# Hybrid mLSTM / attention step on one core: a run's additions placed behind the last plain tile, and the first sample state three ticks later

## The chip, the cores and the metric

The kernel runs on one core of a Trainium2 chip. The core has a matrix engine (TensorE, PE in the profile; its weight loads are shown as PEld), VectorE (DVE), ScalarE (ACT), GpSimd (POOL) and SyncE (SP), whose queue issues most of the transfers between DRAM and the on-chip memory. Each engine works through its own instructions in a fixed order; semaphores make it wait for the others. The metric is the device time of one execution in microseconds. Times of a kernel are given as the median of several runs; the profile is of one further execution.

## The reference

One layer of a decoder is computed for 512 prompt positions and 32 sample positions (8 sequences of 4), 544 columns in all, with model width 2048. All arithmetic is in float32.

- u = x w_in gives q, k, v, o and z of the mLSTM branch (4 heads of width 512), q, k, v and z of a sliding-window attention branch, two merge gates and the input and forget gates.
- For the samples, each of the 8 sequences has a state C (512 x 512 for each head), which is read and updated. In the reference this is, for a chunk,

```
num = einsum('bhts,bhsd->bhtd', s, v) + inter * einsum('bhtk,bhkv->bhtv', q, C)
C_new = decay * C + einsum('bhsk,bhsv->bhkv', w * k, v)
```
- Each branch is normalised and gated (br_m, br_a), then y = sigmoid(g_m) * (br_m w_proj_m) + sigmoid(g_a) * (br_a w_proj_a), and the result is the layer norm of alpha * x + y w_out. The new states are outputs too.

## The kernel before, in words

**Products in float32.** PE multiplies in a narrower format. A weight tile of 128 x 1024 (half of the depth of one column tile) is loaded as `raw`, ScalarE casts it to the high part `wh` (L200) and VectorE subtracts, `wl = raw - wh` (L201, both in `split`). The activations have such parts too. A product is made of high x high, high x low and low x high. Buffers: three of `raw`, two of each of `wh` and `wl`.

**Plain column tiles** (`gemm`, `products`, matmuls at L209): two halves, in each 8 steps of the depth, with three products on two column halves of 272: 48 matmuls for each half. In each step of the depth the matmuls with `wh` come first, then the one with `wl`.

**Runs of pairs** (`paired`, L697). Two column tiles are computed with a seven-product scheme of the Strassen-Winograd kind: seven steps n = 0 to 6, each with 16 matmuls on a `wh` (L664) and 8 on a `wl` (L666). The weight operands of the steps are sums of the four quarter blocks b11, b12, b21, b22 of the weights. `prepare` makes them up to three steps ahead, at raised scheduling priority: in n = 1 it adds t1 = b11 + b12, in n = 2 it adds b11 = t1 + b22 (both VectorE, L644), other sums are made by accumulating transfers of POOL (L642); then it splits the sum. `gather` combines the seven results. There are three runs: one for w_in (about 102 to 1785 us), one for w_proj_m (from about 2160) and one for w_out (from about 2337). Ahead of the second and the third, four column tiles go through plain `gemm`; while these run, `operand_sums` makes the sums of the activations for the run behind them (L1548 to L1551 and the casts and subtractions L243, L244 on s1, n2, n3, s4), and `merge` (L1577, L1578) multiplies finished plain tiles by the gate.

**Ticks.** Each step of a run of pairs, and each part of a plain gemm, ends with `tick()`, which moves a list of generators on by one `yield`. One of them is `samples()`, which works through the samples of the mLSTM heads during the first run.

**The sample chain.** For each head, `sample_prep` loads q, k, v, replicates them (L1087, L1110), transposes them on PE (L1096, L1115), writes the scaled k and the v through a DRAM buffer (`d_kv`, L1060) and loads them back in another layout as KB (L1066) and VB (L1067); nT (L1127, L1129) and the normaliser's products (L1133) are made here too. Then `sample_head` (L1173) takes the eight states: POOL masks KB into Ab (L1192), some ticks pass (`for j in range(4 + b % 2): yield`, L1197), in which the stores of the last state and the loads of the next C are issued; PE multiplies the masked q by C (L1211, four matmuls) and Ab by VB (L1216, four), at a priority that puts them ahead of other work of that tick; VectorE updates C (L1218, four). `sample_finish` normalises (L1162, L1169) and stores the head to `d_brm` (L1171). When the last of four heads is through, `samples()` closes its buffers and loads the 16 tiles `pf` of the attention branch (L1246), which are split into bh and bl (L243, L244).

**After the first run** the plain gemm of w_proj_a multiplies these bh and bl, with the prompt's mLSTM (`mlstm`, whose d_v, d_k and d_q loads are at L1463) between its ticks, up to about 2070 us; then come the four plain tiles of w_proj_m and the second run.

**What sets the order.** A scheduler lays the program's instructions out on each engine by priority and by the order in which the program issues them; `tc.high_priority(offset=n)` moves a block forward, and `tc.issue_after(ins)` puts what is traced in its block behind `ins` in the order of the engine of `ins`.

Of the kernel before, what the change touches and what calls it, by code (L numbers as in the profile page):

```python
# [18 lines left out]
ALU = mybir.AluOpType  # L19
# [55 lines left out]
def _build(tc, nc, i, o, es):  # L75
# [11 lines left out]
    V, A, G, PE = nc.vector, nc.scalar, nc.gpsimd, nc.tensor  # L87
# [13 lines left out]
    def nm(s):  # L101
        count[0] += 1
        return f"{s}_{count[0]}"
# [7 lines left out]
    def r32(ap):  # L111
        return ap.bitcast(F32)
# [13 lines left out]
    state = {}  # L126

    def tick():

        with ExitStack() as place:  # L130
            if state.get("end"):
                place.enter_context(tc.issue_after(state["end"].ins))
            for g in list(live):
                if next(g, StopIteration) is StopIteration:
                    live.remove(g)
# [58 lines left out]
    def split(raw, p=None, tags=("wh", "wl"), parts=1):  # L194
        p = p or wp
        wh = p.tile([128, 8, 128], F32R, tag=tags[0], name=nm("wh"))
        wl = p.tile([128, 8, 128], F32R, tag=tags[1], name=nm("wl"))
        n = 8 // parts
        for k in range(0, 8, n):
            A.copy(wh[:, k:k + n], raw[:, k:k + n])  # L200
            V.tensor_tensor(out=wl[:, k:k + n], in0=raw[:, k:k + n], in1=r32(wh[:, k:k + n]), op=ALU.subtract)  # L201
        return wh, wl

    def products(ps, half, wh, wl, xh, xl, cols, every=8):
# [110 lines left out]
    for g in range(8):  # L315
        for q in range(2):
            k = g * 2 + q
# [311 lines left out]
    def load_a(w):  # L629
        w["b11"], w["b12"] = (load_half(w["wv"], c0, 0) for c0 in (w["cA"], w["cB"]))  # L630

    def load_b(w):
        for n, c0 in (("b22", w["cB"]), ("b21", w["cA"])):
            w[n] = raw2()
            state["load"] = nc.sync.dma_start(w[n][:], w["wv"][:, 8:16, c0:c0 + 128])

    def prepare(w, n):


        def add(out, a, b):  # L640
            if w.get("acc") and out == a and n != 2:
                G.dma_start(out=w[out][:], in_=w[b][:], accum_op=ALU.add)  # L642
            else:
                V.tensor_tensor(out=w[out][:], in0=w[a][:], in1=w[b][:], op=ALU.add)  # L644
        if n == 1:
            w["t1"] = raw2()
            add("t1", "b11", "b12")
        elif n == 2:
            add("b11", "t1", "b22")
        w["hl", n] = split(w[("b11", "t1", "b11", "b21", "b12", "b22", "b21")[n]])  # L650
        if n == (1 if w.get("acc") else 3):
            add("b12", "b12", "b22")
        elif n == (3 if w.get("acc") else 4):
            add("b21", "b21", "b11")

    def half_product(w, n):
        if n < 3:
            w["bank", n] = bank()
        ps = w["bank", BANK[n]][:, :HT]
        wh, wl = w.pop(("hl", n))  # L660
        x, first = w["x"][n], n in (0, 1, 2)
        for k in range(8):
            for p in range(2):
                PE.matmul(ps, wh[:, k], x(p, k), start=(first and k == 0 and p == 0), stop=False, skip_group_check=True)  # L664
        for k in range(8):
            state["end"] = PE.matmul(ps, wl[:, k], x(0, k), start=False, stop=(k == 7), skip_group_check=True)  # L666

    def gather(w, n):

        A0, D0, B0 = (w["bank", b][:, :HT] if ("bank", b) in w else None for b in range(3))  # L670
        sc = w["scale"]
        if n == 0:
            w["p1"] = pe_.tile([128, HT], F32, tag="p1", name=nm("p1"))
            A.activation(w["p1"][:], A0, AF.Copy, scale=sc)
            return
        if n == 1:
            w["O1"], w["O2"] = ev(), ev()
        c11, c21 = (w["O1"][:, c:c + HT] for c in (0, HT))
        c12, c22 = (w["O2"][:, c:c + HT] for c in (0, HT))
        p1 = w["p1"][:]  # L680
        if n == 1:
            A.activation(c11, D0, AF.Copy, scale=sc)  # L682
            G.tensor_tensor(out=c22, in0=p1, in1=c11, op=ALU.subtract)  # L683
        elif n == 2:
            V.scalar_tensor_tensor(c12, B0, sc, p1, op0=ALU.mult, op1=ALU.subtract)
        elif n == 3:
            A.activation(c11, A0, AF.Copy, scale=sc)
        elif n == 4:
            V.scalar_tensor_tensor(c22, B0, -sc, c22, op0=ALU.mult, op1=ALU.add)  # L689
        elif n == 5:  # L690
            V.scalar_tensor_tensor(c12, D0, sc, c12, op0=ALU.mult, op1=ALU.add)
        else:
            V.scalar_tensor_tensor(c21, B0, sc, p1, op0=ALU.mult, op1=ALU.subtract)

    AHEAD = 400

    def paired(work):  # L697

        steps = [(w, n) for w in work for n in range(7)]
        ready = 0  # L700
        with tc.issue_after(state["load"].ins):
            load_a(work[0])
            load_b(work[0])
        for at, (w, n) in enumerate(steps):

            while ready < min(at + 3, len(steps)):
                with tc.high_priority(offset=AHEAD):
                    prepare(*steps[ready])
                ready += 1
            p = at // 7 + 1  # L710
            if p < len(work):
                if n == 3:
                    load_a(work[p])
                elif n == 4:
                    load_b(work[p])
            if n == 2 and "early" in w:
                w["early"]()
            half_product(w, n)
            with tc.high_priority(offset=AHEAD):
                gather(w, n)  # L720
            if n == 6:
                w["end"](w["O1"], w["O2"])
            tick()
# [346 lines left out]
    def load_C(h, b):  # L1070
        ct = sp["sC"].tile([128, 4, 512], F32, tag="C", name=nm("C"))
        nc.sync.dma_start(ct[:], i["state_mlstm_C"][b, h].rearrange("(c p) v -> p c v", p=128))
        return ct
# [99 lines left out]
    def sample_head(h):  # L1173
        r = {}
        nxt = load_C(h, 0)
        yield from sample_prep(h, r)
        pC, stores = None, []

        def store():

            with tc.issue_after(state["load"].ins):
                for dst, src in stores:
                    nc.sync.dma_start(dst, src)
            stores.clear()

        for b in range(NB):
            ct = nxt

            if b % 2 == 0:
                kb, vb = r["kv"]  # L1190
            Ab = st1([128, 128], "Ab", F32R, "sw")
            masked = G.tensor_scalar(Ab[:], r32(kb[:]), cc[:, C_M2 + b % 2:C_M2 + b % 2 + 1], None, op0=ALU.mult)  # L1192
            qz = st1([128, 4, NS], "qz", p="sw")
            with tc.issue_after(masked.ins):
                G.memset(qz[:], 0.0)
            G.tensor_copy(qz[:, :, b * 4:b * 4 + 4], r["qs"][:, :, b * 4:b * 4 + 4])
            for j in range(4 + b % 2):  # L1197
                yield
                if j == 0:
                    store()  # L1200
                elif j == 2 and b + 1 < NB:
                    with tc.issue_after(state["load"].ins):
                        nxt = load_C(h, b + 1)
                        if b % 2:
                            r["kv"] = load_kv(h, b // 2 + 1)
            if b == 0:
                pC = bank()

            with tc.high_priority(offset=3000):
                for c in range(4):  # L1210
                    PE.matmul(pC[c * 32:c * 32 + 32, :], qz[:, c], ct[:, c],  # L1211
                              start=(b == 0), stop=(b == NB - 1), tile_position=(0, c * 32))
                pus = [sm() for _ in range(4)]
                for c in range(4):
                    own = slice(c * 32, c * 32 + 32)
                    PE.matmul(pus[c][:], Ab[own], vb[own], start=True, stop=True, tile_position=(c * 32, 0))  # L1216
            for c in range(4):
                V.scalar_tensor_tensor(ct[:, c], ct[:, c], dcb[:, h, b:b + 1], pus[c][:], op0=ALU.mult, op1=ALU.add)  # L1218
                if c % 2:
                    stores.append((C_s[b, h, (c - 1) * 128:c * 128 + 128, :].rearrange("(c p) v -> p c v", p=128),  # L1220
                                   ct[:, c - 1:c + 1]))
            yield
        yield
        store()
        while h not in gated:
            yield
        yield from sample_finish(h, r, pC)
# [597 lines left out]
    for g in range(G3):  # L1825
# [13 lines left out]
        for half, raw in enumerate(raws):  # L1839
            wh, wl = (w[:, :, g] for w in w3[half])  # L1840
# [54 lines left out]
```

## Time and profile before

| | |
|---|---|
| median of 3 runs | 2493.77 us (2491.63 to 2494.89) |
| the profiled execution | 2497.55 us, its span 2495.7 us |
| TensorE busy | 2453.8 us (98% of the span) |
| VectorE busy | 1817.8 us (73%) |
| ScalarE busy | 1244.1 us (50%) |
| mean granted clock of TensorE | 0.995 |
| moved by DMA | 464.71 MB, mean 186 GB/s |

How to read the rows below. A row of waits names the engine, its operation and what it waited for, then the sum in us, how often, and the longest. A row of a timeline has the start in us from the beginning of the span, the busy time in us of the instructions grouped in it, the engine, the line, the operation, output and inputs with their shape, and the count; square brackets hold the idle time of the engine in front of it and what ended it. Matmuls overlap, so the distance between starts, not the busy time, is their pace. A row of windows has the stretch, its length, the busy time of PE, PEld, DVE, ACT and POOL with instruction counts, the granted clock, the share of the DMA engines and GB/s. A row for one line or tile has the count, the least, median and greatest duration in ns, and the first and last start.

### The profile page before, as it was taken

What the parts mean: (1) busy time and instruction counts of PE and PEld (TensorE: products, weight loads), DVE (VectorE), ACT (ScalarE), POOL (GpSimd) and SP (SyncE); (2) the same over time, 40 slices, a digit from 0 to 9 for tenths busy, and PEclk for the clock granted to TensorE, in tenths of its full rate; (3) what the DMA queues carried; (4) which work ended last, traced back from release to release, by engine and by line L of the source; (5) the groups of instructions that cost most, each with busy time, mean ns of one, the idle gap of its engine ahead of it and who ended that gap; (6) DMA issues with size and microseconds to landing.
All of it is one profiled execution on the core that took longest, in us unless ns stands there. A gap on an engine that the chain in (4) does not pass through costs nothing. (4 is left out here: it accounts for less than half of the span.)

```text
span 2495.7 us, 48772 instructions
## 1 busy us (share of the span) xinstructions
PE 2453.8 (98%) x19542; PEld 2394.0 (96%) x19542; DVE 1817.8 (73%) x2785; ACT 1244.1 (50%) x2033; POOL 373.1 (15%) x376
## 2 busy tenths in 40 slices
PE   8999999999999999999999999999999999999997
PEld 8999999999999999989999999999999999999997
DVE  7867677677677677777878788878855654666667
ACT  6457677667667665433433444444633333334431
POOL 2111121121111111121021121210000000110111
PEclk9999999999999999999999999999999999999999
DMA  6677666656666655468678677677755546788776
GB/s 166 154 185 187 150 151 159 158 144 163 153 152 156 151 128 151 106 204 243 205 216 243 167 232 240 188 225 226 251 171 172 189 149 205 198 229 258 213 220 190
DMA packets 557172, 464.71 MB, mean 186 GB/s; under 512 B 45328, under 2 KB 454080, under 8 KB 556688
## 3 DMA queue, kind: packets, MB, share of 16 engines
q1 hardware_dynamic: 540048, 402.07, 54.4%
q0 software_dynamic: 15696, 57.15, 11.8%
q8 instruction: 154, 2.52, 0.4%
q10 hardware_dynamic: 1200, 2.36, 0.3%
q14 instruction: 74, 0.61, 0.1%
HBM read 319.06 MB, written 96.31 MB: 166 GB/s over the span
## 5 line engine op out<-in xcount | busy, mean ns | idle before, releaser
L200 ACT CAST wh<-raw 128x1024 fp32r<-128x1024 f32 x632 | 661.9, 1048 | 814.6 <-PE bank L664 663.8
L201 DVE TENSOR_TENSOR wl<-raw,wh 128x1024 fp32r<-128x1024 f32 x632 | 778.9, 1234 | 222.7 <-ACT wh L200 203.4
L664 PE MATMUL bank<-xk,wh 128*128 128x272 f32 x2336 | 325.0, 290 | 0.9 <-DVE ev L689 0.9
L644 DVE TENSOR_TENSOR raw<-raw,raw 128x1024 f32<-128x1024 f32 x238 | 304.5, 1280 | 17.3 <-DMA raw<-in_w_in 8.2
L664 PEld LDWEIGHTS bank<-xk,wh 128*128 128x128 f32 x2336 | 304.3, 189 | 4.2 <-issue 2.6
L683 POOL TENSOR_TENSOR ev<-p,ev 128x272 f32<-128x272 f32 x82 | 124.8, 1522 | 674.1 <-ACT ev L682 613.7
L666 PE MATMUL bank<-xk,wl 128*128 128x272 f32 x1168 | 172.4, 288 | 0.8 <-DVE wl L201 0.8
L664 PE MATMUL bank<-s1h,wh 128*128 128x272 f32 x656 | 169.1, 291 | 0.2 <-ACT wh L200 0.2
L664 PE MATMUL bank<-n3h,wh 128*128 128x272 f32 x656 | 169.1, 289 | 0.0
L664 PE MATMUL bank<-n2h,wh 128*128 128x272 f32 x656 | 168.2, 289 | 0.6 <-ACT wh L200 0.6
L664 PE MATMUL bank<-s4h,wh 128*128 128x272 f32 x656 | 168.3, 290 | 0.1
L664 PE MATMUL bank<-n3l,wh 128*128 128x272 f32 x656 | 167.9, 287 | 0.0
L664 PE MATMUL bank<-n2l,wh 128*128 128x272 f32 x656 | 167.5, 287 | 0.0
L664 PE MATMUL bank<-s1l,wh 128*128 128x272 f32 x656 | 167.2, 287 | 0.0
L664 PE MATMUL bank<-s4l,wh 128*128 128x272 f32 x656 | 167.0, 287 | 0.0
L666 PEld LDWEIGHTS bank<-xk,wl 128*128 128x128 f32 x1168 | 156.6, 188 | 1.1 <-DVE wl L201 1.0
L664 PE MATMUL bank<-a11h,wh 128*128 128x272 f32 x584 | 150.8, 290 | 2.6 <-ACT wh L200 2.5
L209 PE MATMUL bank<-bh,wl 128*128 128x272 f32 x704 | 148.5, 291 | 4.7 <-DVE wl L201 4.7
L664 PE MATMUL bank<-a11l,wh 128*128 128x272 f32 x584 | 149.6, 289 | 0.0
L209 PE MATMUL bank<-bh,wh 128*128 128x272 f32 x704 | 148.8, 290 | 0.0
L209 PE MATMUL bank<-bl,wh 128*128 128x272 f32 x704 | 148.6, 290 | 0.0
L664 PEld LDWEIGHTS bank<-n3h,wh 128*128 128x128 f32 x656 | 123.3, 188 | 1.9 <-issue 1.4
(488 smaller groups left out, 5515.4 us busy)
## 6 DMA issues: line engine op xcount, KB each, us to landing
raw<-in_w_in SPq DMA_DIRECT2D x296, 512.0 KB
raw<-raw POOLq DMA_DIRECT2D x90, 512.0 KB, 5.0
C<-in_state_mlstm_C SPq DMA_DIRECT2D x32, 1024.0 KB
out<-C SPq DMA_DIRECT2D x64, 512.0 KB
raw<-in_w_proj_a SPq DMA_DIRECT2D x32, 512.0 KB
raw<-in_w_proj_m SPq DMA_DIRECT2D x32, 512.0 KB
raw<-in_w_out SPq DMA_DIRECT2D x32, 512.0 KB
d_v<-ev SPq DMA_DIRECT2D x16, 272.0 KB
```

The source lines that it names most:

```text
L200: A.copy(wh[:, k:k + n], raw[:, k:k + n])
L201: V.tensor_tensor(out=wl[:, k:k + n], in0=raw[:, k:k + n], in1=r32(wh[:, k:k + n]), op=ALU.subtract)
L209: PE.matmul(ps[f][:, :w], a[:, kk], b(k, c, w), start=(k == 0 and n == 0), stop=(k == 15 and n == 2))
L644: V.tensor_tensor(out=w[out][:], in0=w[a][:], in1=w[b][:], op=ALU.add)
L664: PE.matmul(ps, wh[:, k], x(p, k), start=(first and k == 0 and p == 0), stop=False, skip_group_check=True)
L666: state["end"] = PE.matmul(ps, wl[:, k], x(0, k), start=False, stop=(k == 7), skip_group_check=True)
L683: G.tensor_tensor(out=c22, in0=p1, in1=c11, op=ALU.subtract)
```

## The change

There are two edits.

1. `split` keeps its last subtraction in `state["split"]`. `paired` reads it on entry, when it is the subtraction of the last half of the last plain tile, and wraps `prepare` in `tc.issue_after` of that instruction. The additions and subtractions that `prepare` issues on VectorE stand behind it.
2. In `sample_head` the loop of ticks in front of the state's matmuls has 7 passes instead of 4 for the first state of the first head (`h + b == 0`). All other states keep 4 or 5.

```
-            V.tensor_tensor(out=wl[:, k:k + n], in0=raw[:, k:k + n], in1=r32(wh[:, k:k + n]), op=ALU.subtract)
+            state["split"] = V.tensor_tensor(out=wl[:, k:k + n], in0=raw[:, k:k + n], in1=r32(wh[:, k:k + n]),
+                                             op=ALU.subtract)
...
-        ready = 0
+        ready, plain = 0, state["split"]
...
-                with tc.high_priority(offset=AHEAD):
+                with tc.high_priority(offset=AHEAD), tc.issue_after(plain.ins):
                     prepare(*steps[ready])
...
-            for j in range(4 + b % 2):
+            for j in range(7 if h + b == 0 else 4 + b % 2):
                 yield
```

## The prediction, on record before the changed kernel ran

> **What bounds the kernel now.** I read the page first, then the list of what TensorE waited for, then the timelines of each engine round the longest waits.
>
> ```profile
> span 2495.7 us, 48772 instructions
> PE 2453.8 (98%) x19542; PEld 2394.0 (96%) x19542; DVE 1817.8 (73%) x2785; ACT 1244.1 (50%) x2033; POOL 373.1 (15%) x376
> ```
> PE works 2453.8 of 2495.7 us. The change removes no PE work (it moves instructions only), so it can win only in the 41.9 us that PE idles and in work done at a lower clock. The waits of PE say where (the start of the kernel and the tail behind the last matmul, which the change leaves alone, are left out here; us in total, times, longest):
>
> ```profile
> PE sm L1216 <- DMA VB<-d_kv: 5.4, 2, 5.1
> PE bank L209 <- DVE wl L201: 4.7, 2, 4.0
> PE bank L666 <- DVE wl L201: 0.8, 1, 0.8
> PE sm L1133 <- DVE nT L1129: 0.8, 1, 0.8
> ```
> The first two rows hold the two places that the change touches, 9.1 us. The other two are the next in size on its path, 0.8 us each.
>
> **Part 1: the run's additions behind the last plain tile's subtraction.** TensorE and VectorE just ahead of the second run of pairs (w_proj_m), from their timelines:
>
> ```profile
> 2147.64 0.41 PE L209 MATMUL bank<-bl,wh 128*128 128x272 f32 x2
> 2152.07 0.82 PE L209 MATMUL bank<-bh,wl 128*128 128x272 f32 x2 [4.02 <-DVE wl L201]
> 2152.69 0.66 PE L209 MATMUL bank<-bh,wh 128*128 128x272 f32 x2
> 2157.17 0.41 PE L209 MATMUL bank<-bl,wh 128*128 128x272 f32 x2
> 2159.92 0.29 PE L664 MATMUL bank<-bh,wh 128*128 128x272 f32 x1
> ```
> ```profile
> 2144.09 0.44 DVE L244 TENSOR_TENSOR n3l<-tx,n3h 128x272 fp32r<-128x272 f32 x1
> 2148.61 1.23 DVE L644 TENSOR_TENSOR raw<-raw,raw 128x1024 f32<-128x1024 f32 x1 [4.08 <-DMA raw<-in_w_proj_m]
> 2149.75 0.78 DVE L1577 TENSOR_TENSOR c<-bank,c 128x272 f32<-128x272 f32 x2
> 2150.45 0.43 DVE L1551 TENSOR_TENSOR tx<-tx 128x272 f32<-128x272 f32 x1
> 2150.80 1.22 DVE L201 TENSOR_TENSOR wl<-raw,wh 128x1024 fp32r<-128x1024 f32 x1
> ```
> ```profile
> 2143.74 1.05 ACT L200 CAST wh<-raw 128x1024 fp32r<-128x1024 f32 x1
> ```
> VectorE stands idle 4.08 us in front of the addition L644 (t1 = b11 + b12), which waits for a weight load; behind it in the queue stand L1577, L1551 and the subtraction L201 whose wl PE needs from 2148.05 on. The wh of that half was ready at 2144.79. In the changed kernel's VectorE order this one L644 stands behind that L201. Then L1577, L1551 and L201 follow n3l: 2144.5 + 0.7 + 0.35 + 1.2 = 2146.8 us, 1.2 us before PE wants wl. The 4.02 us go. The clock goes with them: from 2152.07 to 2157.17 the spacing of matmul pairs is 0.45 us instead of 0.25. Those 11 pairs take 5.10 us and would take 11 x 0.25 = 2.76, so 2.3 us more. **Part 1: -6.3 us.**
>
> What is late next: L644 itself still ends at 2149.8, and behind it the split of n=0 (buffers free at about 2148, wh to 2149.1, wl to 2151.0). PE would begin the run at 2159.92 - 6.3 = 2153.6 and need n=0's wl 2 us later and t1's split 3 us later; so 2 us or more are spare. In the third run (w_out) the same move of one L644 is made where PE has no gap, worth nothing; in the first run VectorE's order stays. No DMA and no instruction of SP, POOL, ACT or PE moves by part 1.
>
> The Trainium skill, "TensorE: Matmul & The Clock Gate", section "Part 1: The HAM clock gate", says that the clock is halved after an idle window of about 3.4 us and released after one busy window of the same length. By that the work behind the gap would lose at most half of 3.4, 1.7 us, and part 1 would be -5.7; the trace has 5.1 us of half clock and decides, by its rows, for -6.3.
>
> **Part 2: the first state of the first head three ticks later.** A tick is one step of the run of pairs (24 matmuls, 3.0 us). PE there, then SP:
>
> ```profile
> 1075.82 1.06 PE L1211 MATMUL bank<-C,qz 128*32 128x512 f32 x8
> 1081.94 0.89 PE L1216 MATMUL sm<-VB,Ab 32*128 32x512 f32 x4 [5.05 <-DMA VB<-d_kv]
> 1082.76 3.42 PE L664 MATMUL bank<-xk,wh 128*128 128x272 f32 x16
> 1096.05 2.18 PE L664 MATMUL bank<-xk,wh 128*128 128x272 f32 x16
> 1260.47 0.50 PE L1216 MATMUL sm<-VB,Ab 32*128 32x512 f32 x4 [0.31 <-DMA VB<-d_kv]
> ```
> ```profile
> 1073.91 0.54 SPq L1067 DMA_DIRECT2D VB<-d_kv  x1
> 1253.92 0.54 SPq L1067 DMA_DIRECT2D VB<-d_kv  x1
> 1427.54 0.54 SPq L1067 DMA_DIRECT2D VB<-d_kv  x1
> 1606.01 0.56 SPq L1067 DMA_DIRECT2D VB<-d_kv  x1
> ```
> VB is issued at 1073.91 and lands when PE goes on, 1081.94: 8.0 us. PE reaches L1216 at 1076.89. With three steps between, it gets there at 1076.89 + 9 = 1085.9, 4 us behind the landing. The gap of 5.05 us goes, and with it the half clock: 3.42 - 2.18 + 0.89 - 0.50 = 1.6 us. **Part 2's gain: -6.7 us.**
>
> The three ticks move everything that follows in the sample chain, on every engine, up to the end of the mLSTM stage. By the two programs' orders all first states shift by 3 steps (300, 353, 406, 459 to 303, 356, 409, 462), but the preparations of the heads do not shift alike: from the transposition L1115 to the first state there were 3.0, 5.2, 5.5, 5.1 steps and are 6.0, 5.5, 4.0, 5.2.
>
> ```profile
> L1115 PE MATMUL sm<-cc,rep x4: 270/272/273, 1064.8 to 1065.1; 128*128 128x128 f32 x4
> 1417.63 0.60 PE L1115 MATMUL sm<-cc,rep 128*128 128x128 f32 x4
> 1422.16 0.42 PE L1133 MATMUL sm<-nT,qs 128*32 128x8 f32 x8 [0.77 <-DVE nT L1129]
> ```
> - Head 2. L1216 stands 3.0 x steps + 3.1 us behind L1115 (head 0: 1076.89 - 1064.8 = 12.1 = 9.0 + 3.1), so at 15.1 us. VB was issued 1427.54 - 1417.63 = 9.9 us behind L1115 in this head, and lands 6.5 (1253.92 to 1260.4) to 8.0 us later: 16.4 to 17.9, a wait of 1.3 to 2.8. The other heads' issues (8.8 to 12.4 us behind) give 0.2 to 5.3, the last with a half clock worth 2 more. I take 1.5, near its own lower end.
> - Head 3. Its L1133 stands 0.8 steps behind L1127, where 0.9 gave the 0.77 us above and 1.2 gave none. 0.77 + 0.1 x 3.0 = 1.1; ends 0 and 1.5. I take 1.
> - Gone: the 0.31 us of head 1 (0.3 steps more), the 0.77 of head 2 (L1133 has 1.6 steps now), and the 0.70 below: -1.8, ends 0 and -2.5.
>
> **Where the delay can come back: the start of w_proj_a.** When the last head is done, SP loads 16 tiles of the attention branch (pf), which this gemm multiplies.
>
> ```profile
> L1169 PE MATMUL sm<-cc,w x4: 221/222/243, 1764.0 to 1764.2; 32*128 32x32 f32 x4
> 1766.39 0.37 SPq L1171 DMA_DIRECT2D d_brm<-gs  x1
> 1766.86 9.97 SPq L1246 DMA_DIRECT2D pf<-d_bra x16
> 1777.64 1.50 SPq L187 DMA_DIRECT2D raw<-in_w_proj_a  x2
> ```
> ```profile
> 1770.24 0.64 ACT L243 CAST bh<-pf 128x544 fp32r<-128x544 f32 x1
> 1784.78 0.41 PE L209 MATMUL bank<-bh,wh 128*128 128x272 f32 x2
> 1786.14 0.52 PE L209 MATMUL bank<-bh,wl 128*128 128x272 f32 x2 [0.70 <-DVE wl L201]
> 1770.00:1780.00 10.00, 10.00 (x82) 10.00 (x81) 9.07 (x11) 6.07 (x9) 1.45 (x1) 1.00 1.00 362
> ```
> Call the start of w_proj_a T (1784.78). L1169 stood 20.8 us ahead of T, and the order puts it 2.8 steps, 8.4 us, ahead now. The first pf issue follows it by 2.9 us, its landing by 3.4 more: T - 2.1, its cast ends at T - 1.5. The 16 issues take 9.97 us, 0.62 each; at 362 GB/s a 278 KB tile takes 0.77 us. PE uses up one tile in 6 matmuls, three pairs of 0.25 us, 0.75. So the loads run level with PE at a lead of 1.5 us, and in the same stretch the casts of pf share ScalarE with the second tile's wh. I take 2 us of waiting; ends 0 and 6. The mLSTM chunks behind find their d_v and d_k loads behind pf as well; I take 1, ends 0 and 3.
>
> The Trainium skill, "DMA: Bandwidth & Descriptors", section "Queues, rings and completion order", says that each DMA engine consumes a queue's descriptors in ring order. That speaks against the change: the two weight loads that came behind pf now stand ahead of it on SP's queue. By it the sum would be up to 2.9 us worse (below).
>
> **The sum.** -6.3 - 6.7 - 1.8 + 1.5 + 1 + 2 + 1 = -9.3 us. Against the profiled execution's own 2497.55 us that is 2488.2. This execution was 3.8 us over the median 2493.77 (span plus 1.9 us around it), so in the medians' terms **2484.5 us**, -0.37%. About 0.2%, 5.0 us, is what a measurement of this kernel can tell from no change: 2488.8 and 2498.8.
>
> **The rivals.**
> 1. *The waits come back elsewhere.* Head 2's VB lands at the late end (5.3 us and a half clock of 2), and the two weight loads, 1.05 MB at 362 GB/s = 2.9 us, are still under way when pf is issued, so that PE waits 2 + 2.9 there: -6.3 - 6.7 - 1.8 + 7.3 + 1 + 4.9 + 1 = -0.6, 2493.2. One of the two alone gives 2487.4 to 2490.3. For it: 0.3 steps between safe and late in head 1's row. Against: the two weight buffers are read for the last time some 10 us before T, so their loads may be over.
> 2. *Slower: state updates in front of subtractions.* Every state moves three steps within the seven-step pair, and VectorE's order with it. Four updates take 3.0 us:
> ```profile
> L1218 DVE SCALAR_TENSOR_TENSOR C<-C,dcb,sm 128x512 f32<-128x512 f32 x128 | 87.8, 741 | 5.2 <-PE sm L1216 4.1
> ```
> If they come to stand ahead of a wl that has less than 3.0 us to spare, PE waits once in each state, by the nearest row (L666 for wl) 0.8 us: 31 x 0.8 = 25 us, 2484.5 + 25 = 2509.5. From some 18 of such waits on the kernel is slower beyond the bound. Against it: 32 states pass now with one such wait in all, in two phases (4 and 5 ticks), so several positions have been met without harm.
> 3. *It does not do what it says.* PE at 2148 finds another input late (t1's split, n=0), or VB is issued later with the delay; the gaps shrink by less than half: 2488 to 2494.
>
> **How the numbers follow.** Forecast 0.62 (2479 to 2488.8); rival 1 0.20 (a quarter of it still under 2488.8); rival 2 0.07; rival 3 0.05; pf later than every bound above 0.06 (half of it slower). Faster 0.62 + 0.05 = 0.67; slower 0.07 + 0.03 = 0.10; same 0.23. The range: all new costs at nothing and the small waits gone give -13 - 2.5 = 2478.3; upward it takes in rival 1 to 2493.5. What is left out is rival 2, most of the last case and what lies under the low end, near 0.15.
>
> **What would show it.** Part 1: no PE wait for wl before the second run, PEclk full there, L644 behind L201. Part 2: no wait at the first L1216, its VB landed 4 us earlier; about 1.5 us at head 2's first L1216 and 1 us at head 3's L1133; a first pf issue 5.5 us ahead of w_proj_a, and some 2 us of PE waits for bh or wh in its first 20 us. Wrong would be a gap over 3 us at either place, a new PE wait at each state, or w_proj_a starting with a gap of 5 us.

## The result, and the profile after

| | before | after |
|---|---|---|
| median of 7 runs | 2491.63 us (2488.45 to 2495.76) | 2483.67 us (2480.84 to 2487.65) |
| profiled execution | 2497.55 us, span 2495.7 | 2483.67 us, span 2481.7 |
| ratio of the runs | | 0.9969, 95% interval 0.9959 to 0.9978 |

The change makes the kernel 7.7 us faster by the ratio (0.31%), 8.0 us by the two medians. The forecast was 9.3 us, the predicted 2484.5 us lies 0.8 us above the median. The two profiles differ by more, 14.0 us of span; why they do is the main finding of the experiments.

The page of the changed kernel. Lines of its code from 203 on have numbers one higher than before.

```profile
span 2481.7 us, 48772 instructions
PE 2448.2 (99%) x19542; PEld 2390.0 (96%) x19542; DVE 1813.4 (73%) x2785; ACT 1244.7 (50%) x2033; POOL 372.7 (15%) x376
```
PE executes the same 19542 instructions and is busy 5.6 us less (2453.8 before). Most of that is work no longer done at half clock, 3.9 us by the rows that the prediction shows for the two places. The other 8.4 us of the span are idle time of PE that has gone. From its list of waits (us in total, times, longest), the two longest behind the start, which here means the first 110 us; the others there are 0.7 us or less:

```profile
PE sm L1217 <- DMA VB<-d_kv: 1.1, 1, 1.1
PE bank L210 <- DVE bl L245: 0.9, 1, 0.9
```
The 5.1 us for VB and the 4.0 us for wl are gone. What is left for VB is one wait of 1.1 us, in another place (below), and 0.9 us for bl is new.

Part 1's place, the end of the last plain tile before the second run, on VectorE, then two windows of it (PE, PEld, DVE, ACT and POOL busy, granted clock, DMA share, GB/s):

```profile
2137.80 1.21 DVE L201 TENSOR_TENSOR wl<-raw,wh 128x1024 fp32r<-128x1024 f32 x1
2142.36 1.23 DVE L645 TENSOR_TENSOR raw<-raw,raw 128x1024 f32<-128x1024 f32 x1 [3.34 <-DMA raw<-in_w_proj_m]
```
```profile
2139.00:2143.00 4.00, 4.00 (x34) 4.00 (x33) 0.66 (x2) 1.05 (x1) 0.00 (x0) 1.00 0.85 238
2143.00:2147.00 4.00, 4.00 (x34) 4.00 (x33) 3.97 (x6) 0.48 (x1) 0.94 (x1) 1.00 0.48 124
```
VectorE still stands 3.34 us in front of the addition and still waits for the same load, but the subtraction is through already, at 2139.0, 2 us before PE needs its wl (2141.0); PE works all 8 us, at a clock of 1.00. The wait has not been removed, it has been moved to where nobody waits for VectorE.

Part 2's place, the first state of the first head, then the first state of head 2:

```profile
1085.27 1.06 PE L1212 MATMUL bank<-C,qz 128*32 128x512 f32 x8
1086.26 0.50 PE L1217 MATMUL sm<-VB,Ab 32*128 32x512 f32 x4
1440.61 0.50 PE L1217 MATMUL sm<-VB,Ab 32*128 32x512 f32 x4 [1.14 <-DMA VB<-d_kv]
```
The first L1217 follows L1212 without a gap. Head 2 waits 1.14 us for its VB, where 1.5 had been reckoned.

The start of w_proj_a, on SP and PE:

```profile
1770.84 10.97 SPq L1247 DMA_DIRECT2D pf<-d_bra  x16
```
```profile
1777.38 0.50 PE L210 MATMUL bank<-bh,wh 128*128 128x272 f32 x2
1781.59 0.52 PE L210 MATMUL bank<-bl,wh 128*128 128x272 f32 x2 [0.86 <-DVE bl L245]
```
The first pf load is issued 6.5 us ahead of the gemm (5.5 had been reckoned), and PE waits once, 0.86 us.

### The profile page after: what moved, and what is told of

Same layout as the page of the kernel before. It is cut to its first block, busy times and chain, and to the rows that moved or that the text cites. A ratio compares the mean times of both kernels' runs of the same rounds, so it can differ in the third digit from the quotient of the medians.

```text
span 2481.7 us, 48772 instructions
## 1 busy us (share of the span) xinstructions
PE 2448.2 (99%) x19542; PEld 2390.0 (96%) x19542; DVE 1813.4 (73%) x2785; ACT 1244.7 (50%) x2033; POOL 372.7 (15%) x376
## 4 chain that ended last, share of the span: by engine, by line
PE 94%; DVE 2%; DMA 2%; ACT 1%; issue 0%; SPq 0%; POOL 0%; DVEq 0%; ACTq 0%; POOLq 0%
PE bank L665 45%; PE bank L667 22%; PE bank L210 13%; PE sm L1400 2%; PE bank L1212 1%; PE sm L1432 1%; PE sm L773 1%; PE sm L1445 1%; PE sm L811 1%; PE sm L210 1%; PE sm L801 1%; DMA raw<-in_w_in 1%; PE sm L1762 1%; PE sm L1217 1%; DVE wl L201 0%
## 5 line engine op out<-in xcount | busy, mean ns | idle before, releaser
L665 PE MATMUL bank<-xk,wh 128*128 128x272 f32 x2336 | 324.1, 289 | 1.9 <-DVE ev L690 1.9
L665 PEld LDWEIGHTS bank<-xk,wh 128*128 128x128 f32 x2336 | 303.1, 188 | 5.5 <-issue 2.6
L665 PE MATMUL bank<-s1h,wh 128*128 128x272 f32 x656 | 169.0, 291 | 0.1
L665 PE MATMUL bank<-n3h,wh 128*128 128x272 f32 x656 | 168.8, 289 | 0.1
L665 PE MATMUL bank<-s4h,wh 128*128 128x272 f32 x656 | 168.3, 290 | 0.1
L665 PE MATMUL bank<-n2h,wh 128*128 128x272 f32 x656 | 168.2, 289 | 0.0
L665 PE MATMUL bank<-n3l,wh 128*128 128x272 f32 x656 | 168.0, 287 | 0.0
L665 PE MATMUL bank<-n2l,wh 128*128 128x272 f32 x656 | 167.6, 287 | 0.0
L665 PE MATMUL bank<-s1l,wh 128*128 128x272 f32 x656 | 167.1, 287 | 0.0
L665 PE MATMUL bank<-s4l,wh 128*128 128x272 f32 x656 | 167.0, 287 | 0.0
L665 PE MATMUL bank<-a11h,wh 128*128 128x272 f32 x584 | 150.6, 289 | 2.5 <-ACT wh L200 2.5
L665 PE MATMUL bank<-a11l,wh 128*128 128x272 f32 x584 | 149.8, 289 | 0.0
L643 POOL DMA_DIRECT2D raw<-raw x90 | 77.8, 864 | 319.4 <-DVE sums L786 142.8
```

## The experiments

All times are medians on one chip for each group of four kernels, and the ratio is to the kernel before, run on that chip.

**Each half alone, and both kernels again.** `part1_alone` has only the `issue_after` of the additions:

```
+        ready, plain = 0, state["split"]
...
+                with tc.high_priority(offset=AHEAD), tc.issue_after(plain.ins):
...
             for j in range(4 + b % 2):
```


> Part 1 alone (additions of the run behind the last plain tile's subtraction, all states with 4 or 5 ticks). Theory (two separate gaps, each gone with its half clock): PE's wait for wl ahead of the second run goes from 4.0 us to 0, the granted clock there is full, the wait at the first L1216 stays at about 5 us; 6.3 us less than before, ratio 0.9975. Rival (the gap ahead of the second run is as long as 4 us only in some executions, since it hangs on when a weight load lands): the profile shows the gap gone, but the median gains 1 to 3 us, ratio 0.999. Rival (the two parts help each other): under 1 us.

`part2_alone` has only the ticks:

```
                 with tc.high_priority(offset=AHEAD):
...
+            for j in range(7 if h + b == 0 else 4 + b % 2):
```


> Part 2 alone (first state of the first head three ticks later, the additions as before). Theory: the wait of 5.05 us at the first L1216 and its half clock go, 6.7 us; old waits of 0.3 and 0.8 us go, one of about 1.1 us comes at head 2's first L1216; in all 6 to 7 us less than before, ratio 0.9974; PE's wait for wl ahead of the second run stays at about 4 us. Rival (this gap hangs on when VB lands and is shorter in most executions): median gain of 1 to 3 us, ratio 0.999. Rival (the delay is paid back at the start of w_proj_a): a gain at the first state and 2 us or more of new waits at the start of w_proj_a.

The unchanged kernel:

> The kernel before once more, for a second profile and for what two equal kernels differ by. Theory (both gaps belong to every execution): waits of about 5 us at the first L1216 and about 4 us for wl ahead of the second run again, span 2490 to 2496 us. Rival (the one profile of before was an execution with long gaps): one of the two waits is under 2.5 us, or its half clock is absent, span 2487 to 2490. Times against before: no difference, ratio 0.9985 to 1.0015.

The changed one:

> The changed kernel once more, beside its two halves. Theory (gains add): ratio 0.995 to 0.997, neither of the two waits in the profile, about 1 us at head 2's first L1216, under 1.5 us in all at the start of w_proj_a. Rival (the profile of after was an execution with short new waits): new waits of 3 us or more in all at head 2, head 3 and the start of w_proj_a.

| kernel | median us | ratio to before (95%) | first L1216/7 waits | wl ahead of run 2 |
|---|---|---|---|---|
| before | 2491.82 | | 5.05 | 4.02 |
| before_again | 2491.48 | 0.9995 (0.9986 to 1.0005) | 4.21 | 1.28 |
| part1_alone | 2490.94 | 0.9995 (0.9986 to 1.0004) | 4.49 | none |
| part2_alone | 2485.47 | 0.9975 (0.9965 to 0.9984) | none | 2.35 |
| both_again | 2483.76 | 0.9968 (0.9956 to 0.9980) | none | none |

The waits are each from one profile; those of before are from the profile shown first. Part 2 does what was reckoned. Part 1 takes its wait away, yet its median gains 0.9 us (by the ratio 1.2, from 3.5 us faster to 1.0 slower), not 6.3: this fits the first rival of its expectation. The gain is not lost again behind the wait: from the start of the second run to the end the profiles of before, `before_again`, `part1_alone` and the changed kernel take 335.2 to 335.8 us. Nor does the second rival show, that the halves help each other: their gains by the ratios add to 7.4 us (1.2 and 6.2), against 8.0 for `both_again`. The wait in front of the second run is not a constant of the kernel, as the rival in the expectation of `before_again` had it. The second profile of the unchanged kernel, on PE and by windows:

```profile
2149.70 0.52 PE L209 MATMUL bank<-bh,wl 128*128 128x272 f32 x2 [1.28 <-DVE wl L201]
```
```profile
2149.00:2153.00 4.00, 3.30 (x26) 3.30 (x27) 3.97 (x6) 0.91 (x1) 0.00 (x0) 1.00 0.90 134
```
The same wait is 1.28 us here, and the clock stays at 1.00 behind it. With it this execution's span is 2490.8 instead of 2495.7 us.

**A third profile of before, and what makes the wait vary.**

> A third profile of the kernel before. Theory (the first gap belongs to every execution, the second varies with the landing of a load): 4 to 5 us at the first L1216, and for wl ahead of the second run anything from 0.5 to 4 us. Rival (4 us is the rule there): 3.5 us or more.

Its median was 2492.55 us, ratio 1.0003 (0.9992 to 1.0014). PE, and the windows behind the wait:

```profile
2152.47 0.82 PE L209 MATMUL bank<-bh,wl 128*128 128x272 f32 x2 [4.48 <-DVE wl L201]
```
```profile
2151.00:2155.00 4.00, 2.54 (x11) 2.54 (x12) 3.96 (x7) 1.36 (x2) 0.74 (x1) 0.50 0.75 118
```
So three profiles of one kernel have 4.02, 1.28 and 4.48 us there, with spans of 2495.7, 2490.8 and 2495.9; 5 us between them are about 3 us of wait and 2 of half clock. Taken alone, this third profile fits the rival of its expectation (3.5 us or more) and not the theory (0.5 to 4); that about 4 us is not the rule rests on the 1.28 us, on the 2.35 us of `part2_alone`, which has the same order there, and on the small gain of part 1. The first L1216 waits 5.05, 4.21 and 5.02 us in the same three profiles and 4.49 in `part1_alone`: that one was there in every profile without part 2.

SP in the first profile of before shows where the variation comes in:

```profile
2134.44 1.73 SPq L1588 DMA_DIRECT2D d_y<-c  x1
2142.60 0.34 SPq L1573 DMA_DIRECT2D c<-d_t  x1
2143.03 0.39 SPq L187 DMA_DIRECT2D raw<-in_w_proj_m  x1
```
The last row is b12, for which the addition L644 waits. It stands behind a load c<-d_t, and that one waits until the store d_y<-c has landed, since it overwrites the stored buffer. From the end of the store's issue to the load of c are 6.4 us here and 4.9 in `before_again` (2136.49 to 2141.38); b12's own landing takes 5.6 us here and 4.4 there. In `before_third` the two are 6.2 and 5.6 us. Two transfers in a row, each a little longer, put 2.4 us on the addition; why they are longer is not shown.

`weights_first` tests this: the unchanged kernel, with the additions where they were, but with the run's weight loads ahead of the loads of d_sgm and d_t on SP.

```
-        w["b11"], w["b12"] = (load_half(w["wv"], c0, 0) for c0 in (w["cA"], w["cB"]))
+        w["b11"], w["b12"] = (load_half(w["wv"], c0, 0) for c0 in (w["cA"], w["cB"])); state["a"] = state["load"]
...
-            merges.extend(merged(c) for c in (ct, ct + 1))
+            with tc.issue_after(state["a"].ins): merges.extend(merged(c) for c in (ct, ct + 1))
```


> The kernel before, with one thing changed: the two loads of the gate and of d_t for the first pair of a run stand behind the run's weight loads on SP instead of between them. The addition L644 still stands ahead of the last plain tile's subtraction. Theory (the gap ahead of the second run is the landing of b12, whose load stands on SP behind a load c<-d_t that waits for a store to land): b12 is issued about 4 us earlier, when its buffer comes free, L644 ends at least 1.2 us ahead of the last subtraction's need, and PE's wait for wl ahead of the second run is under 0.5 us although the order that part 1 changes is the old one. Rival (the load itself is slow, whatever it stands behind): a wait of 1.3 to 4 us stays. Median: 1 to 3 us less than before, as part 1 alone.

Median 2492.70 us, ratio 0.9998 (0.9989 to 1.0006). SP, then VectorE:

```profile
2138.24 0.37 SPq L187 DMA_DIRECT2D raw<-in_w_proj_m  x1
2138.66 0.57 SPq L1572 DMA_DIRECT2D c<-d_sgm  x1
2139.32 0.46 SPq L1573 DMA_DIRECT2D c<-d_t  x1
```
```profile
2142.57 1.22 DVE L644 TENSOR_TENSOR raw<-raw,raw 128x1024 f32<-128x1024 f32 x1
2144.07 0.78 DVE L1577 TENSOR_TENSOR c<-bank,c 128x272 f32<-128x272 f32 x2
2144.76 1.21 DVE L201 TENSOR_TENSOR wl<-raw,wh 128x1024 fp32r<-128x1024 f32 x1
```
b12 is issued when its buffer comes free and not behind c<-d_t; the addition is done at 2143.8 and the subtraction behind it, in the old order, at 2146.0, in time by 0.5 us (PE comes to its wl at 2146.5). PE has no wait there. Where the wait comes from is shown by this, in one profile, and the change's part 1 is one of two ways around it. Part 1 is the safer one: all nine profiles of kernels that have it are without this wait. The median gains nothing that can be told from zero, as with part 1 alone, so in a usual execution the wait costs little, about 1 us, and at most 3.5 by the interval of part 1; how long it usually is was not measured. Two of the three profiled executions of before lie high (2497.55 and 2497.79 us against medians of about 2492). Whether by chance is not shown, but a steady offset of profiled executions does not show either: the 13 that are among the timed runs of their kernel lie between 3.5 us under and 5.2 us over its median.

**The number of ticks.** `one_tick` and `two_ticks` are the changed kernel with a smaller delay, `six_ticks` with a larger one, `head2_later` has one more tick for head 2:

```
-            for j in range(7 if h + b == 0 else 4 + b % 2):
+            for j in range(5 if h + b == 0 else 4 + b % 2):
...
+            for j in range(6 if h + b == 0 else 4 + b % 2):
...
+            for j in range(10 if h + b == 0 else 4 + b % 2):
...
+            for j in range(7 if h + b == 0 else 5 if h == 2 and b == 0 else 4 + b % 2):
```


> As changed, but the first state of the first head one tick (3 us) later than before instead of three. Theory (a gap is what PE arrives early, and the clock halves only for a long one): a wait of 5.05 - 3.0 = 2 us is left at the first L1216, and the clock behind it stays full; so 2 us slower than the changed kernel there. Rival (the half clock comes with any wait at this place): 2 us and 1.6 more. Head 2 has 5.0 steps between L1115 and the first state instead of 4.0 and should not wait.

> As changed, but two ticks later than before instead of three. Theory: PE reaches the first L1216 at 1076.9 + 6 = 1082.9, 1 us behind VB's landing, so no wait there; head 2 has 4.0 steps as in the changed kernel and waits about 1 us; head 1 has 4.9 steps and 17.8 us from L1115 to L1216, with VB there 6.5 us behind an issue that came 12.4 us behind L1115: about 1 us. In all the same as the changed kernel within 2 us. Rival (three ticks are needed because SP or POOL come later too): a wait of 1 us or more at the first L1216.

> As changed, but six ticks later than before instead of three. The last head's L1169 then stands 0.8 steps, 2.4 us, ahead of the end of the first run instead of 8.4. Theory (each us that the last head comes later is taken from the pf loads' lead, 1.5 us or less by now): the first pf is issued 1 us behind the start of w_proj_a, lands at 4.4, and PE waits there 4 to 6 us, with half a clock for 3 to 7 us behind it: 6 to 9 us slower than the changed kernel, less the 1.1 us at head 2 (5.5 steps there). Rival (pf is hidden or another input comes first): under 2 us there.

> As changed, and the first state of head 2 one more tick later (5.0 steps from L1115 to the first state instead of 4.0). Theory: head 2's wait at L1216 (1.1 us) goes; the last head's L1169 moves 1.3 steps nearer to the end of the first run, 4.4 us ahead of it, so the first pf is issued about 1 us ahead of w_proj_a and lands 2.5 us behind its start: 3 us of waiting there; in all 1 to 3 us slower than the changed kernel. Rival (the loads have room): 1 us faster.

| kernel | median us | ratio to before (95%) | waits of PE behind the start, over 1 us |
|---|---|---|---|
| one_tick | 2487.41 | 0.9975 (0.9963 to 0.9986) | 1.51 first L1217; 1.22 and 2.23 L665 for ev |
| two_ticks | 2488.45 | 0.9975 (0.9965 to 0.9985) | 2.65 head 2's L1217 |
| six_ticks | 2499.61 | 1.0025 (1.0015 to 1.0035) | 2.65 head 1's L1217; 11.52 w_proj_a |
| head2_later | 2488.86 | 0.9979 (0.9969 to 0.9989) | 4.23 w_proj_a |

The kernel before had a median of 2494.16 us on this chip, and the changed kernel was not in this group; against its ratios from the other groups (0.9969, 0.9968 and 0.9959) all four medians are slower, but only that of `six_ticks` clearly: the intervals of the other three overlap those of the changed kernel.

- `one_tick`: the wait that is left at the first state is 1.51 us (2 expected), with a clock of 1.00 behind it, as the theory had it. Not foreseen were two waits for ev, at 1586.7 and 1638.1 us, of a kind that the changed kernel has only at its start. The longer one, on VectorE and PE:

```profile
1637.48 0.44 DVE L686 SCALAR_TENSOR_TENSOR ev<-bank,p 128x272 f32<-128x272 f32 x1 [6.43 <-DMA d_sgm<-ev]
```
```profile
1638.07 0.39 PE L665 MATMUL bank<-n3h,wh 128*128 128x272 f32 x1 [2.23 <-DVE ev L686]
```
VectorE waits 6.43 us for a store to free the buffer ev, and PE waits for VectorE to free the bank; 0.57 is the granted clock in the 4 us behind it. In nine of the other 13 profiles VectorE waits for such a store too, 2.7 us at most and with no wait of PE behind it; whether the one-tick shift made this store late, or this execution did, a single profile does not show.
- `two_ticks`: no wait at the first state, as the theory had it, but 2.65 us at head 2, where about 1 was expected; its VB was issued at 1432.23, 11.0 us behind its transposition (L1115 before, L1116 here), and landed 6.9 us later.
- `head2_later`: head 2's wait goes, and 4.23 us come at w_proj_a instead (3 expected).
- `six_ticks`: 11.52 us at w_proj_a, twice what was expected. PE and SP there:

```profile
1792.70 0.82 PE L210 MATMUL bank<-bh,wh 128*128 128x272 f32 x2 [11.52 <-ACT bh L244]
```
```profile
1777.91 0.52 SPq L1172 DMA_DIRECT2D d_brm<-gs  x1
1778.48 3.20 SPq L1464 DMA_DIRECT2D t<-d_q  x4
1782.08 0.32 SPq L1273 DMA_DIRECT2D d_sga<-ev  x1
1782.67 0.32 SPq L1519 DMA_DIRECT2D c<-d_sga  x1
1783.43 1.28 SPq L187 DMA_DIRECT2D raw<-in_w_proj_a  x2
1784.76 12.58 SPq L1247 DMA_DIRECT2D pf<-d_bra  x16
```
The last head's store stands 3.3 us ahead of the gemm (1781.18 is where PE stops), and pf was expected 1 us behind the gemm's start. But eight other transfers of the next stage stand between the store and pf on SP: pf is issued 6.85 us behind the store, 3.6 us behind the gemm's start. The price of a later head is thus not 1 us for 1 us; the loads fall behind others in the queue. The mechanism of the expectation holds, its size does not.

**A version that keeps both gains and gives the lead back.** `recover` is the changed kernel with one more tick at head 2's first state and one less at the four odd states of the last head:

```
-            for j in range(7 if h + b == 0 else 4 + b % 2):
+            for j in range(7 if h + b == 0 else 5 if h == 2 and b == 0 else 4 + (b % 2 if h < 3 else 0)):
```


> As changed, and the first state of head 2 one tick later, and the four odd states of the last head with 4 ticks instead of 5, so that the last head's L1169 stands at the step where it stood before (504.2, 20 us ahead of the end of the first run). Theory (the new costs of the change are head 2's VB and the pf loads' lead): head 2's wait of 1.1 to 1.7 us and the wait for bl at the start of w_proj_a go, the old 0.7 us for wl there may come back; 1 to 3 us less than the changed kernel, ratio to before 0.9960. Rival (the shorter ticks of the last head make its loads of C or VB late): waits of 1 us or more at L1211 or L1216 of head 3, no gain.

> The changed kernel beside the one above: ratio to before 0.9960 to 0.9975; about 1 us at head 2's first L1216 and under 1 us at the start of w_proj_a.

| kernel | median us | ratio to before (95%) |
|---|---|---|
| recover | 2482.55 | 0.9958 (0.9943 to 0.9972) |
| both_third | 2484.19 | 0.9959 (0.9945 to 0.9973) |

The waits move as expected: `recover` has none for VB, and the old one of 0.7 us for wl at the start of w_proj_a is back, where `both_third` has 1.97 us at head 2. The span less PE's busy time is 32.8 against 33.5 us. In the runs the two can't be told apart: what is left there is under what the measurement shows.

## Why the prediction was right, and where it was not

**The net was right; several terms were not, and they cancel.** By the steps of the sum:

- *Part 1, -6.3.* Between the two profiles it came: up to the last plain tiles the changed kernel is 6.9 us ahead, at the start of the second run 13.4 us (2146.52 instead of 2159.92), so 6.5 us are won in between. The step that failed is "the 4.02 us go", as a statement on the median. It took the gap of one execution for that of the kernel. Three profiles of before have 4.02, 1.28 and 4.48, and over the runs part 1 is worth about 1 us (1.2 in `part1_alone`, 1.7 as the difference of the medians of `part2_alone` and `both_again`). The mechanism is right, the term is some 5 us too large, and at least 2.8 by the interval of `part1_alone`; the sign of the gain on the median is not shown by the runs. The prediction knew that its profiled execution lay 3.8 us over the median, and carried that as an offset without asking which of its own terms might be those 3.8 us.
- *Part 2's gain, -6.7.* Right as far as the runs tell: `part2_alone` gains 6.2 us (0.9975; 4.0 to 8.7 by the interval) as the net of this gain, of the small waits that are gone (2.4, below) and of its new wait of 1.5 us at head 2, where 6.7 + 2.4 - 1.5 = 7.6.
- *Head 2, +1.5.* Right: 1.14, 1.51, 1.65 and 1.97 us in four profiles. The term was worked out as steps between L1115 and the state, against the issue and landing of VB; in the changed kernel PE comes to the state 15.1 us behind the transposition, as reckoned, and VB is issued 9.6 us behind it and lands 6.6 us later; `two_ticks` (2.65 at 4.0 steps) and `six_ticks` (2.65 at head 1, 4.2 steps) show the same mechanism.
- *Head 3, +1.* Wrong: no wait. The distance on PE was read about rightly; the step that failed is that this distance decides. In head 2 of before PE came to L1133 at 1421.39, 3.2 us behind L1127, and waited 0.77 us; in head 3 of the changed kernel L1134 stands 3.2 us behind L1128 and does not wait. What differs is when VectorE comes to nT, 3.75 us behind L1127 there and 0.45 us behind L1128 here (first row: VectorE in head 2 of before; the others: head 3 of the changed kernel):

```profile
1421.91 0.19 DVE L1129 COPY nT<-sm 128x32 f32<-128x32 f32 x1
1598.91 0.41 PE L1128 MATMUL sm<-cc,w 8*128 8x8 f32 x4
1599.36 0.19 DVE L1130 COPY nT<-sm 128x32 f32<-128x32 f32 x1 [0.65 <-PE sm L1128]
1602.07 0.42 PE L1134 MATMUL sm<-nT,qs 128*32 128x8 f32 x8
```
- *The start of w_proj_a, +2.* Right in kind, 0.86 us in size. The lead of pf was 6.5 us and not 5.5, and the two weight loads were issued 5.8 us ahead of pf (1765.02 and 1770.84), so their coming first cost nothing that shows. `head2_later` and `six_ticks` show that the change sits close to the edge: one tick more costs 4.23 us there.
- *mLSTM order, +1.* 0.3 us: w_proj_a begins 7.4 us earlier than before and the stage ends 6.9 us earlier, of which the waits at its start (0.86 for 0.70) are 0.2.
- *Gone, -1.8.* The waits of 0.31, 0.77 and 0.70 us are gone, and the 0.64 us for wh of n2 behind head 2's first state too.

With part 1 at its measured 1 us and the new costs at theirs, the sum is -1.2 - 6.7 - 2.4 + 1.1 + 0.9 + 0.3 = -8.0, against -7.7 measured. So the forecast of -9.3 came near because a gain 5 us too large met costs 3 us too large; that is luck.

**The rivals.** The first (the waits come back elsewhere) is what happens at one tick more, not here. The second (updates in front of subtractions in every state) did not show: PE has no repeated wait for wl in any profile; `one_tick` alone has two waits of a like kind, for ev. Its row was misread: the wait of 0.8 us at L666, taken there as the one wait in 32 states and above as lying on the change's path, is at 69.8 us, in the first steps of the first run (which begins at about 58 us and not at 102); of the 32 states before the change none had such a wait. The third (the change doesn't do what it says) is false in the profile; for the median of part 1 it is nearly true, for a reason that it did not name.

**The clock.** Behind the start the 14 profiles agree on two things: every wait over 4 us was followed by half clock, and none under 2 us was. Between them the length alone did not decide. Two rows, with waits of 2.35 us in `part2_alone` and 2.65 us in `two_ticks`:

```profile
2143.00:2147.00 4.00, 3.60 (x18) 3.61 (x19) 3.97 (x6) 0.61 (x1) 0.00 (x0) 0.63 0.97 156
```
```profile
1439.00:1443.00 4.00, 3.86 (x31) 3.62 (x32) 3.33 (x5) 1.05 (x1) 0.77 (x1) 1.00 0.24 88
```
Behind the shorter wait the clock fell to 0.63 in the window, behind the longer one it stayed at 1.00 (`six_ticks` has one of 2.65 us too, with 0.67 behind it). In the start even less was enough in some profiles. All 14 have a wait for wh between 102 and 106 us, of 1.69 to 2.20 us; in seven of them the clock of the next 4 us was 0.57 to 0.67 (waits of 1.83 to 2.20), in the other seven it was 1.00 (waits of 1.69 to 2.15). The waits and windows of `part2_alone`, then of `both_third`:

```profile
102.41 0.39 PE L665 MATMUL bank<-a11h,wh 128*128 128x272 f32 x1 [1.98 <-ACT wh L200]
103.00:107.00 4.00, 4.00 (x22) 4.00 (x21) 3.94 (x8) 0.00 (x0) 0.00 (x0) 0.59 0.84 248
```
```profile
103.94 0.39 PE L665 MATMUL bank<-a11h,wh 128*128 128x272 f32 x1 [1.95 <-ACT wh L200]
104.00:108.00 4.00, 4.00 (x32) 4.00 (x33) 3.94 (x8) 0.00 (x0) 0.00 (x0) 1.00 0.97 285
```
What decides there is not shown. The Trainium skill's rule, "TensorE: Matmul & The Clock Gate", section "Part 1: The HAM clock gate", has a window of about 3.4 us. The rows do not agree with it as a threshold: a wait that is shorter than the rule's window can cost clock too.

## What to carry to other kernels

Before a gap is priced from one profile, ask what ends it: a gap that ends with two transfers in a row (a store that has to land, then a load) varies from run to run, and a second profile of the unchanged kernel costs less than the wrong term. When a wait can't be shortened, look at what stands behind it in the engine's order; moving the waiting instruction behind the urgent one removed the gap here as an earlier load did, and with more to spare (2 us against 0.5). When a chain is delayed, count the distance of its last transfers to their user and what else will be queued ahead of them: three ticks brought 2 us of new waits here, a fourth at head 2 cost 4.23 us at the far end.

## What the runs showed that was not expected

- One kernel's executions differ by 5 us through one wait: 1.28 us with a clock of 1.00 behind it, or 4.48 us with 0.50. Of 74 runs of the unchanged kernel in the two groups with both halves and with `weights_first`, 14 took 2495 us or more; of the 11 runs of `part1_alone` none did (at most 2493.76 us), of the 12 of `weights_first` one (2495.46). In the third group, on a chip whose median is 2 us higher, it was 13 of 35. This fits a long wait in a fifth of the executions or more, which both remedies take away; with so few runs of the remedies it is not shown, and the runs without a profile don't show which wait it was.
- In `one_tick` a store was late for its buffer's next use at 1638 us and PE waited 2.23 us, which no other profile has; that the ticks at 1082 us caused it is not shown.
- The order on SP cost more than the delay itself: with three more ticks the pf loads came 6.85 us behind the store that they follow at once (0.5 us) in the kernel before (`six_ticks`).
